# A hybrid decoder layer on one core: projections 256 tokens at a time and a pair of blocks ahead, their weights through a ring, the gate's products moved

## The chip, the cores and the metric

The kernel runs on one core of a Trainium2 chip. A core has TensorE (PE in the profile; its weight loads are PEld), VectorE (DVE), ScalarE (ACT), GpSimd (POOL) and SyncE (SP), which issues most DMA transfers. Each engine works its own instructions in a fixed order and waits on semaphores for the others. The metric is the device time of one execution in microseconds, as a median of runs. The time before is 2795.03 us (three runs, 2791.49 to 2799.54).

## The reference

One decoder layer over 2048 tokens of width 1024, in float32, with two sandwich-normalised sub-layers:

```
xn   = rms_norm(x) * g
proj = xn @ w_in                                   # 3336 columns
z, xbc, dt = SSD part (512, 1024, 8 columns)
xbc  = silu(causal_conv4(xbc));  dt = softplus(dt + bias)
y_ssd  = chunked state-space scan (8 heads of 64, 2 groups, state 128), times silu(z), group norm
p    = p_rwkv + (shift_by_one_token(p_rwkv) - p_rwkv) * mu     # 1792 columns: r, w_lo, k, v, a_lo, g_lo
S_t  = S_{t-1} * w_t + (S_{t-1} a_t) b_t + v_t k_t ;  y_t = S_t r_t   # RWKV7, 8 heads of 64, per token
h    = x + rms_norm([y_ssd ; y_rwkv] @ w_out)
y    = h + rms_norm( (silu(gate) * val) @ w_down ),  gate, val = causal_conv3(rms_norm(h) @ w_up)
```

All mixing is causal.

## The kernel before, in words

The work is written in three phases, R, S and F, that hand data to one another through DRAM: XN (the normed tokens, transposed), XC (the convolved xbc columns), YR (the RWKV output), H and HN. Every large product is done in two-term half precision: a float32 operand is split into a high and a low float16 part, and three products (high-high, high-low, low-high) are summed in PSUM. So a product over the 1024 features is 8 x 3 = 24 matmuls.

**Phase R** goes over 16 blocks of 128 tokens. For a block, `load` (L302) fetches x, norms and transposes it into `xt`, whose first three columns are the last three of the block before, and stores it to XN. The projections are 14 groups of 128 columns for RWKV (`d`, L330, weights `W`) and 8 groups for xbc (`conv`, L349, weights `WC`). All weights are split once at the start and stay in SBUF. `dense` (L200) issues the 24 matmuls; they move 129 columns for `d` (128 tokens and the one before, for the token shift) and 131 for `conv` (three before, for the 4-tap convolution). After every second group ACT and DVE take the pair out of PSUM: `d` makes a token-shift mix (L342 to L347), `conv` makes the taps (one on POOL at L362, three on DVE at L367), a tanh and a product (L372), and a store to XC.

The recurrence of a block is done in 64-token halves in matrix form: `low_rank`, `keys`, `norm` (with product nq, L412), `receptance`, `gram` (two, L443, masked into G at L447), `solve` (L451) and `transposed`; these belong to the front of the block (`f.`). `solve` inverts triangular 32 x 32 blocks: the blocks of G go to DRAM (ATd) and come back redistributed over the partitions (atl), 62 small DVE operations at L471 and L474 do the substitution, and the result goes through DRAM (XTd) to XT. The back of a block (`b.`), which runs during the next block's front, is `values`, `own`, `merge` (pw and po; its first step transposes XT into XW at L515), `update` (pu), `state` (pS, pq), `gate` and `finish` (yt).

TensorE's order is the order in which the program calls these steps: phase R runs through the step lists FIRST, SECOND, PLAN, LAST and DRAIN. The other engines' orders, and that of the DMA issues, are set by a planner with its own time estimates. In PLAN (L122) the projections `f.d.0` to `f.d.13` and `f.conv.0` to `f.conv.7` of a block are strewn among the front steps of the same block and the back steps of the block before. `merge.0` stands two groups ahead of `gram.0`.

**Phase S** goes over 16 chunks of 128 tokens (pairs of chunks share loads). For a pair, `steps`, `sums` and `flip` make the step sizes dt and their running sums (products dt at L763, acs at L795 and L806; a chain of tiny DVE operations at L774 to L790). For a chunk, `z` (L824) makes the gate's columns in four bursts of six matmuls of 512 columns; then come `begin`, `decay`, `keys`, `off`, `y`, `state`, `norm`, `o` (the output projection, four bursts of 12 at L958) and `post` (the two norms and the transposed copy hT, which goes to HN; product ht at L983). While phase R drains its last block (DRAIN, each "S" is one step of S_DRAIN), it runs chunk 0, the z bursts of chunks 0 to 3 and the steps of pairs 0 and 1. From chunk 1 on, each chunk runs S_PLAN (L100), in which a "Z" is one z burst of a later chunk (from a list that S_QUOTA deals out), and `s.steps`, `t.sums`, `t.flip` are those of a later pair. `post` of a chunk comes one chunk after its `o`.

**Phase F** is the feed-forward part, in two halves of 1024 tokens. The change doesn't touch it.

Of the kernel before, what the change touches and what calls it, by code (L numbers as in the profile page):

```python
# [7 lines left out]
F32 = mybir.dt.float32  # L8
# [46 lines left out]
class Space:  # L55
# [20 lines left out]
R_LEFT = ("sq", "kkn", "thw", "tha", "Pv", "xin", "wl", "wr", "tk", "BK", "ca cth", "raw", "xt", "wc")  # L76
R_RIGHT = (
    "cw cb mus omu w0h a0h ka5 kam tiny vr gnv gnr ss pnv pnr", "XT0 XT1 qs S0_0 S0_1 tS ysb yln tg",
    "g2 cmat tv GL WA WX xl tmp XW", "UV", "G", "BT", "atl", "Pi", "AR", "tr",
)  # L80
S_LEFT = (
    "wdt dtb Ab Db cst_s sng", "wst", "ws0", "ws1", "xt", "ws2", "ws3", "dv de dq ds dtt da nac", "sz", "th", "xbc", "R",
    "Dt", "pp rr ones3 E", "identb mnegb", "Btok", "Xdt", "Xd", "aend dec sgs sgv sgr", "ST0 ST1", "sq", "yt0",
# [12 lines left out]
S_DRAIN = """  # L96
s.steps c.z.0 c.z.1 c.z.2 c.z.3 s.sums n.z.0 s.flip c.rows n.z.1 n.z.2 n.z.3 c.begin m.z.0 c.off c.keys c.decay.0 m.z.1
c.decay.1 m.z.2 m.z.3 t.steps u.z.0 u.z.1 u.z.2 n.rows c.y u.z.3 c.state
# [5 lines left out]
S_QUOTA = (3,) * 12 + (4,) * 3  # L104
# [3 lines left out]
SPLITS = ('AV', 'AV', 'AV', 'GV')  # L108
FIRST = """
f.d.0 f.d.1 f.d.2 f.d.3 f.low_rank f.d.4 f.d.5 f.keys f.d.6 f.d.7 f.d.8 f.norm f.d.9 f.conv.0 f.receptance f.conv.1  # L110
f.conv.2 f.gram.0 f.conv.3 f.gram.1 f.solve f.conv.4 f.conv.5 f.conv.6 f.conv.7 f.transposed.0
n.load.10.11 f.transposed.1 f.d.12 f.d.13
"""
SECOND = """
f.d.0 f.d.1 b.values f.d.2 f.d.3 f.low_rank f.d.4 f.d.5 f.keys f.d.6 f.d.7 f.d.8 b.own.0 f.norm f.d.9 f.receptance
f.conv.0 f.conv.1 f.conv.2 f.conv.3 f.gram.0 b.merge.0 f.gram.1 f.solve b.merge.1 f.conv.4 b.update.0 f.conv.5 b.state.0
f.conv.6 f.transposed.0 b.own.1 f.conv.7 b.update.1 b.state.1 f.transposed.1 n.load.10.11 b.gate f.d.12 f.d.13 b.finish
"""
LAST = """
# [58 lines left out]
def norm_T(tc, K, work, psp, pstag, src, g, dst, col, sfx, between=None, junk=None):  # L178
# [6 lines left out]
    for q in range(2):  # L185
# [14 lines left out]
def dense(tc, ps, w, xt, cols):  # L200

    nc = tc.nc
    n = 0
# [1371 lines left out]
```

## Time and profile before

| | us |
|---|---|
| median of three runs | 2795.03 |
| the profiled execution | 2795.42 |
| its span, first to last instruction | 2793.4 |
| phase R's projections, first to last | 11.5 to about 1006 |
| z bursts, first to last | 1006.7 to 1436.6 |
| o products, first to last | 1077.1 to 1473.5 |
| granted clock, mean | 0.957 |

The profile is one execution. Busy times of one engine may hold overlapping instructions only once, while the mean in nanoseconds is that of one instruction with its whole pipeline; so for matmuls that follow one another the distance of their starts says what one costs. A row of the timeline gives the start, the length, the instruction and, in brackets, how long the engine sat idle before it and what ended that. A row of the waits gives the waiting instruction, the releaser, the total in us, how often, and the longest.

### The profile page before, as it was taken

Reading aid. Unit: us, or ns where it says so; the run is one execution under the profiler, and the core shown is the slowest. Engines: PE = TensorE matmul, PEld = TensorE weight load, DVE = VectorE, ACT = ScalarE, POOL = GpSimd, SP = SyncE. Lnnn points to the kernel's source line nnn. Section 1 sums busy time; section 2 is a strip of 40 time slices with the busy share of each in tenths; the row PEclk is TensorE's granted clock in tenths of the full one; section 3 lists DMA queues with packets and bytes.
Section 4 is the critical chain, followed back from the end, with each engine's and each line's share of the span. In section 5 each row is a group of like instructions: output and inputs, shape, how many; then the busy total and the mean of one; then the engine's idle time right before and its main releaser. Section 6 shows DMA issues by size and latency. Waiting matters only on the chain.

```text
span 2793.4 us, 54157 instructions
## 1 busy us (share of the span) xinstructions
PE 2533.3 (91%) x21458; PEld 1595.1 (57%) x21468; DVE 1942.4 (70%) x3711; ACT 1196.6 (43%) x2448; POOL 1237.7 (44%) x1286
## 2 busy tenths in 40 slices
PE   5898899999989989899898798989988899999998
PEld 5888888888878865455443343434433344444443
DVE  7778767777777766556767858787879744554557
ACT  5455555445555534344444444434344333132132
POOL 5234434434434423333457855657476532132234
PEclk8999999999999989999999899999999999999999
DMA  6212121221211144333355334343434633333243
GB/s 213 52 43 60 47 48 45 52 51 43 60 47 45 40 149 137 107 105 124 136 183 190 126 138 155 136 154 132 151 129 155 226 99 106 102 101 102 86 137 126
DMA packets 261278, 302.62 MB, mean 108 GB/s; under 512 B 133664, under 2 KB 168864, under 8 KB 257696
## 3 DMA queue, kind: packets, MB, share of 16 engines
q1 hardware_dynamic: 259440, 296.54, 33.4%
q8 instruction: 168, 2.75, 0.4%
q10 hardware_dynamic: 1584, 2.63, 0.3%
q14 instruction: 86, 0.70, 0.1%
HBM read 188.11 MB, written 110.99 MB: 107 GB/s over the span
## 4 chain that ended last, share of the span: by engine, by line
PE 42%; DVE 25%; POOL 11%; DMA 8%; issue 8%; ACT 4%; SPq 2%; POOLq 0%; DVEq 0%; ACTq 0%
PE u L1182 16%; PE d L1329 10%; PE d L206 4%; DVE ca L367 3%; PE o L958 3%; DVE xl L474 3%; DVE tmp L471 3%; POOL fa L1087 2%; DMA HN<-hT 2%; DMA atl<-ATd 2%; DVE a L1219 2%; POOL us L1083 1%; PE l L1410 1%; POOL p L1247 1%; DMA ATd<-G 1%
## 5 line engine op out<-in xcount | busy, mean ns | idle before, releaser
L1182 PE MATMUL u<-b,w 128*128 128x512 f16 x3696 | 820.4, 384 | 52.1 <-DVE C L1191 36.5
L1182 PEld LDWEIGHTS <-w 128*128 128x128 f16 x3696 | 365.3, 99 | 503.5 <-issue 80.5
L206 PE MATMUL d<-xt,wr 128*128 128x129 f16 x5376 | 356.3, 230 | 7.2 <-DVE xt L197 5.1
L206 PEld LDWEIGHTS <-wr 128*128 128x128 f16 x5376 | 346.0, 103 | 28.9 <-issue 23.0
L1329 PE MATMUL d<-dw,fa 128*128 128x512 f16 x1512 | 339.8, 384 | 18.3 <-DVE dw L159 17.6
L1329 PEld LDWEIGHTS <-fa 128*128 128x128 f16 x1596 | 158.1, 99 | 222.7 <-issue 34.7
L1191 DVE TENSOR_TENSOR C<-u,C 128x512 f32<-128x512 f32 x220 | 150.6, 685 | 188.6 <-PE u L1182 151.4
L206 PE MATMUL c<-xt,wc 128*128 128x131 f16 x3072 | 201.2, 223 | 0.3 <-ACT tr L344 0.3
L206 PEld LDWEIGHTS <-wc 128*128 128x128 f16 x3072 | 184.7, 98 | 5.8 <-issue 0.7
L367 DVE SCALAR_TENSOR_TENSOR ca<-rc,cw,ca 128x128 f32<-128x128 f32 x384 | 156.5, 440 | 39.9 <-POOL ca L362 38.3
L1338 DVE TENSOR_TENSOR acc<-d,acc 128x512 f32<-128x512 f32 x212 | 139.8, 682 | 57.3 <-PE d L1329 56.6
L1219 DVE SCALAR_TENSOR_TENSOR p<-C,fpar,p 128x1024 f32<-128x1024 f32 x88 | 121.8, 1384 | 70.2 <-ACT p L1217 70.1
L159 DVE SCALAR_TENSOR_TENSOR w<-us,w 128x512 f16<-128x512 f32 x132 | 121.4, 925 | 68.2 <-ACT w L158 67.1
L471 DVE TENSOR_TENSOR tmp<-atl,xl 128x60 f32<-128x60 f32 (+24 forms) x496 | 122.1, 246 | 52.2 <-DMA atl<-ATd 41.9
L1086 ACT ACTIVATE fa<-p 128x512 f16<-128x512 f32 x132 | 79.6, 624 | 177.4 <-DVE p L1223 94.1
L1087 POOL TENSOR_TENSOR fa<-p,fa 128x512 f16<-128x512 f32 x120 | 151.5, 1273 | 3.6 <-ACT fa L1086 3.6
L474 DVE TENSOR_TENSOR xl<-xl,tmp 128x60 f32<-128x60 f32 (+24 forms) x496 | 137.4, 277 | 11.8
L158 ACT ACTIVATE w<-us 128x512 f16<-128x512 f32 x132 | 80.5, 623 | 139.3 <-POOL us L1083 99.9
L1219 DVE SCALAR_TENSOR_TENSOR a<-C,fpar,a 128x1024 f32<-128x1024 f32 x88 | 128.9, 1465 | 4.5 <-ACT a L1217 1.7
L362 POOL TENSOR_SCALAR ca<-rc,cw,cb 128x128 f32<-128x128 f32 x128 | 69.7, 553 | 135.4 <-ACT rc L359 61.7
L1216 POOL COPY C<-fcarry 128x2 f32<-128x2 f32 x88 | 40.9, 467 | 158.4 <-ACT a L1217 77.3
L1221 POOL COPY fcarry<-C 128x2 f32<-128x2 f32 x88 | 34.4, 391 | 169.1 <-DVE C L1191 168.7
(318 smaller groups left out, 4583.9 us busy)
## 6 DMA issues: line engine op xcount, KB each, us to landing
UW<-w SPq DMA_DIRECT2D x154, 256.0 KB
w<-UW SPq DMA_DIRECT2D x154, 256.0 KB
us<-in_w_u_dram SPq DMA_DIRECT2D x44, 512.0 KB
DW<-dw SPq DMA_DIRECT2D x70, 256.0 KB
dw<-DW SPq DMA_DIRECT2D x56, 256.0 KB
hs<-HN SPq DMA_DIRECT2D x48, 256.0 KB
r<-in_w_d_dram SPq DMA_DIRECT2D x10, 1024.0 KB
xin<-in_x_dram SPq DMA_DIRECT2D x16, 512.0 KB
```

Of the source, the lines that this page charges most:

```text
L159: eng.scalar_tensor_tensor(out=lo, in0=src, scalar=scale, in1=hi, op0=ALU.mult, op1=ALU.subtract)
L206: nc.tensor.matmul(ps, w[:, a, kt, :], xt[:, kt, b, cols], start=n == 0, stop=n == 3 * KT - 1)
L367: V.scalar_tensor_tensor(out=acc[:, q], in0=raw[:, q, k:k + 128], scalar=cw[:, g + q, k:k + 1], in1=acc[:, q], op0=ALU.mult, op1=ALU.add)
L471: V.tensor_tensor(out=tmp[:, :m, :n], in0=atl[:, j, j + 1:32].unsqueeze(1).to_broadcast([P, m, n]), in1=xl[:, :m, j:j + 1].to_broadcast([P ...
L474: V.tensor_tensor(out=xl[:, :m, j + 1:32], in0=xl[:, :m, j + 1:32], in1=tmp[:, :m, :n], op=ALU.add)
L958: nc.tensor.matmul(self.po, l, WO[:, v, (kt + 4) % KT, ds_], start=k == 0, stop=k == 23)
L1087: eng.tensor_tensor(out=lo, in0=src, in1=hi, op=ALU.subtract)
L1182: nc.tensor.matmul(bk[at], self.w[i][:, u, k, :], self.half.b[i][:, k, v, :], start=start and n == 0, stop=n == 11, skip_group_check=True)
L1191: V.tensor_tensor(out=o, in0=ps, in1=a, op=ALU.add)
L1219: V.scalar_tensor_tensor(out=a, in0=c[:, 2 - d:1026 - d], scalar=cw[:, g, 2 - d:3 - d], in1=a, op0=ALU.mult, op1=ALU.add)
L1329: nc.tensor.matmul(ps, pairs[m].a[i][:, u, t * P:t * P + P], ws[n][m][:, v, :], start=new and m == 0 and u == v == 0, stop=m == N - 1 and ...
L1338: V.tensor_tensor(out=acc[j][:, t], in0=ps, in1=acc[j][:, t], op=ALU.add)
```

## The change

In phase R the unit is no longer a block but a pair of blocks for the projections. `load` of two blocks fills one `xt` of 256 columns. A generator (`stream`) yields the projections of all pairs as units: half of one group's product, that is four of the eight feature tiles, 12 matmuls of 256 columns. There are 44 units a pair. Tokens before the pair are no longer projected again; the last one or three columns of the raw projections are kept in `carry` and copied in front of the next pair's. Evacuation, token shift, taps and the tanh work on 256 columns. `low_rank`'s token part (WA, GL, WX) moves to the pair (`gates`).

The stream runs ahead: 30 units and one more inside a `load` are issued before block 0 begins, and each block then takes 22 units ("D" in the one PLAN, one of them inside `load` of the block four ahead). FIRST, SECOND and LAST go. In PLAN the back steps come earlier: `merge.0` stands after eight units, before `norm`, and `gram.0` and `gram.1` after five more.

Weights are no longer resident. A ring of 11 tiles ("wr") holds them. For pairs 0 and 1 they are loaded in float32 and split (each takes two tiles, fetched five groups ahead); pair 1 also stores the split tiles to DRAM (WD). From pair 2 on they are loaded split from WD, ten groups ahead. `wl` gets a fourth, zero-filled part, so that both low-rank products use 128 rows.

When the stream ends (in block 14), each "D" becomes a step of phase S: the 64 z bursts of all chunks, with `steps`, `sums` and `flip` of all pairs among them. The gated z is stored to DRAM (SZ) and loaded in `begin`. Chunk 0's remaining steps (S_FIRST) come when phase R is through; S_PLAN loses its Z, s and t steps and keeps the order of the rest.

```diff
-FIRST = ...   -SECOND = ...   -LAST = ...   -S_QUOTA = ...   -S_DRAIN = ...
+S_FIRST = """c.rows c.begin c.off c.keys c.decay.0 c.decay.1 n.rows c.y c.state"""
 S_PLAN = """
-c.begin c.decay.0 Z c.off p.norm c.keys Z c.decay.1 p.o.0.0 Z t.sums p.o.0.1 t.flip Z n.rows q.post.0 c.y c.state
-p.o.1.0 q.post.1 p.o.1.1 s.steps
+c.begin c.decay.0 c.off p.norm c.keys c.decay.1 p.o.0.0 p.o.0.1 n.rows q.post.0 c.y c.state
+p.o.1.0 q.post.1 p.o.1.1
 """
+LEAD = 30
+RING = 11
 PLAN = """
-f.d.0 f.d.1 b.values f.d.2 f.d.3 f.low_rank f.d.4 f.d.5 f.keys f.d.6 f.d.7 f.d.8 b.own.0 f.norm f.d.9 f.receptance f.conv.0 f.conv.1 b.merge.0 f.conv.2 f.gram.0 b.merge.1 f.conv.3 b.update.0 f.gram.1 f.solve f.conv.4 b.state.0 f.conv.5 f.transposed.0 b.own.1 f.conv.6 b.update.1 f.conv.7 b.state.1 f.transposed.1 n.load.10.11 b.gate f.d.12 f.d.13 b.finish
+D D b.values D f.low_rank D D f.keys D b.own.0 D D b.merge.0 f.norm D b.merge.1 f.receptance D b.update.0 D
+b.state.0 D f.gram.0 D f.gram.1 f.solve b.own.1 D D b.update.1 D f.transposed.0 D b.state.1 D f.transposed.1 D b.gate
+n.load D b.finish D
 """
 DRAIN = """
+D D b.values D D b.own.0 D D D D D D D D D D D D D b.merge.0 D D b.merge.1 D b.update.0 D D b.state.0 D b.own.1 D D
+b.update.1 D D b.state.1 b.gate D D D D D b.finish
 """
...
+        def load_w(pair, g):
+            src = w_r[g] if g < 14 else w_c[g - 14]
+            w = wk.tile([P, 2, KT, P], F16, name=f"w{pair}_{g}", tag="wr", bufs=RING)
+            if pair > 1:
+                nc.sync.dma_start(w, WD[g])
+                return w
+            st = wk.tile([P, KT, P], F32, name=f"wf{pair}_{g}", tag="wr", bufs=RING)
+            nc.sync.dma_start(st, src)
+            ...
+            V.scalar_tensor_tensor(out=lo, in0=st, scalar=WS, in1=hi, op0=ALU.mult, op1=ALU.subtract)
+            if pair == 1:
+                nc.sync.dma_start(WD[g], w)
+            return w
...
+            def units(self):
+                ...
+                for g in range(0, NG, 2):
+                    ps = psp.tile([P, 2, 256], F32, name=f"d{self.sf}_{g}", tag="mm", bufs=2)
+                    ...
+                    for q in range(2):
+                        w = self.weights(g + q)
+                        for k in (0, 4):
+                            dense(tc, ps[:, q], w, self.xt, slice(0, 256), range(k, k + 4))
+                            if q and k:
+                                self.done(g, ps)
+                            yield
+            def raw(self, g, ps, k):
+                raw = wk.tile([P, 2, 259], F32, name=f"raw{self.sf}_{g}", tag="raw", bufs=2)
+                V.tensor_copy(raw[:, :, 3 - k:3], carry[:, g:g + 2, 3 - k:3])
+                S.activation(raw[:, :, 3:259], ps, AF.Copy)
+                V.tensor_copy(carry[:, g:g + 2, 3 - k:3], raw[:, :, 259 - k:259])
+                return raw
...
+        def stream():
+            for p in pairs:
+                for n, _ in enumerate(p.units()):
+                    yield
+                    for g in range(n // 2 + 1, n // 2 + 1 + (RING // 2 if p.n < 2 else RING - 1)):
+                        if g < NG:
+                            p.fetch(g)
+                        elif p.n + 1 < PAIRS:
+                            pairs[p.n + 1].fetch(g - NG)
+        def piece():
+            if not over[0]:
+                if next(pieces, pieces) is not pieces:
+                    return
+                over[0] = True
+                for c in reversed(front):
+                    c.close()
+                next(filler)
+            next(filler)
+        for n in range(LEAD):
+            piece()
+            if n in (9, 19):
+                blocks[2 + n // 10].load(piece if n == 9 else None)
...
 # phase S
+            nc.sync.dma_start(SZ[self.n], sz)          # end of z
 ...
+            self.sz = wk.tile([P, 512], F32, name="szl" + cf, tag="sz", bufs=3)   # begin
+            nc.sync.dma_start(self.sz, SZ[self.n])
...
+    for c in chunks:
+        for g in range(4):
+            if c.c == 0 and g == 0 and c.n // 2 + 1 < blocks:
+                pairs[c.n // 2 + 1].load_x()
+            c.z(g)
+            if c.c == 0 and g == 1:
+                c.q.steps()
+            elif c.c == 1 and g == 0:
+                c.q.sums()
+            elif c.c == 1 and g == 2:
+                c.q.flip()
+            if not K.finished:
+                yield
```

More of the change, by code (lines that the diff above doesn't have):

```diff
@@ L375, in low_rank @@
[L375 to L380 removed]
+            def low_rank(self):
+                X, thw, tha, Pi, Pv = self.pair.X, self.thw, self.tha, self.Pi, self.Pv
@@ L991, in phase_S @@
     chunks = [Chunk(n) for n in range(N)]
-    gates = [(n, g) for n in range(4, N) for g in range(4)]
     def follow(n, plan):
-        left = S_QUOTA[n - 1] if n < N else 0
         for step in plan.split():
@@ L1040, in phase_S @@
             pairs[n // 2 + 1].load_b()
-        elif n % 2 and n // 2 + 2 < blocks:
-            pairs[n // 2 + 2].load_x()
         yield from follow(n, S_PLAN)
```

349 lines of the change are left out of this document (172 added, 177 removed).

## The prediction

> **What bounds the kernel now.** I read the page's share of each engine, then the stretches of the span, and then the first stretch closely, since that is where nearly all of the change lies.
>
> ```profile
> PE 2533.3 (91%) x21458; PEld 1595.1 (57%) x21468; DVE 1942.4 (70%) x3711; ACT 1196.6 (43%) x2448; POOL 1237.7 (44%) x1286
> ...
> 0.00:120.00 120.00, 83.55 (x1056) 74.99 (x1056) 92.47 (x205) 63.85 (x127) 50.06 (x52) 0.87 0.44 145
> 120.00:960.00 840.00, 763.82 (x11663) 694.31 (x11664) 628.40 (x1839) 427.88 (x1024) 341.25 (x407) 0.96 0.20 49
> 1070.00:1440.00 370.00, 336.00 (x1907) 190.73 (x1914) 232.91 (x422) 157.45 (x429) 133.58 (x150) 0.97 0.36 118
> ```
>
> Columns: stretch, length, then PE, PEld, DVE, ACT and POOL busy, granted clock, DMA share, GB/s. PE leads everywhere, but in the steady stretch of phase R it idles 76 of 840 us. One period of a 128-token block runs from one norm product (nq) to the next:
>
> ```profile
> L412 PEld LDWEIGHTS nq<-sq,cst x32: 192/192/338, 46.0 to 969.8; 128*128 128x128 f32 x32
> ...
> PE zw L388 <- DVE WX L384: 26.2, 14, 2.7
> PE yt L617 <- POOL ysb L613: 18.0, 13, 1.4
> PE pS L585 <- ACT UV L568: 13.1, 14, 1.7
> PE gr L443 <- DVE BK L427: 8.6, 13, 0.7
> PE pt L191 <- DVE xin L193: 7.9, 12, 0.7
> ...
> 298.40:358.90 60.50, 55.29 (x860) 50.52 (x858) 46.05 (x135) 31.50 (x76) 25.11 (x30) 0.97 0.20 50
> ```
>
> This is its weight load, two per block; 15 periods from 46.0 to 969.8: 61.6 us each. A single period holds 55.3 us of PE and 46.1 of DVE; PE's waits (in total, times, longest) are short and of many causes. Beside PE runs a second chain of nearly the same length, the triangular solve of a block: gram product, mask (G), two trips through DRAM, 62 small DVE operations, two more trips, transposition (XW), merge product (pw).
>
> ```profile
> 490.32 1.16 PE L443 MATMUL gr<-AR,BK 64*128 64x128 f32 x16
> ...
> 494.61 0.68 DVE L447 TENSOR_TENSOR G<-gr,cst 128x512 f32<-128x512 f32 x1
> 502.60 0.19 DVE L471 TENSOR_TENSOR tmp<-atl,xl 128x31 f32<-128x31 f32 x1 [2.38 <-DMA atl<-ATd]
> 532.60 0.25 DVE L474 TENSOR_TENSOR xl<-xl,tmp 128x8 f32<-128x8 f32 x1
> 540.17 0.43 DVE L515 STREAM_TRANSPOSE XW<-XT 32x256 f32<-32x256 f32 x1 [0.76 <-DMA XT<-XTd]
> ...
> 538.34 1.54 PE L206 MATMUL d<-xt,wr 128*128 128x129 f16 x24
> 539.72 2.98 PE L206 MATMUL c<-xt,wc 128*128 128x131 f16 x48
> 542.63 0.69 PE L522 MATMUL pw<-XW,G 32*32 32x32 f32 x32
> 545.50 1.16 PE L443 MATMUL gr<-AR,BK 64*128 64x128 f32 x16 [0.67 <-DVE BK L427]
> 549.80 1.16 PE L443 MATMUL gr<-AR,BK 64*128 64x128 f32 x16
> ```
>
> From the end of gr (491.5) to the end of XW (540.6) are 49.1 us: 3.8 to G's end, 7.3 to the data, 30.2 of solve (that includes some 14 us of other DVE work), 7.7 back. pw starts only 2.0 us after it. So PE sets the period now, and the solve is the next thing late, by 2 us.
>
> **The change, part by part.**
>
> *Wider projections.* Start to start, 24 products of 129 columns take 1.38 us (538.34 to 539.72), 57.5 ns each; 48 of 131 take 2.91 (to 542.63), 60.6. A block has 14 x 24 and 8 x 24: 31.0 us. Products of 256 columns don't occur in this form; a z burst of 512 columns does:
>
> ```profile
> 1219.86 1.47 PE L830 MATMUL z<-ws,xs 128*128 128x512 f16 x6
> 1221.16 1.03 PE L895 MATMUL pf<-ST,xbc 128*128 128x256 f32 x4
> ```
>
> 1.30 us for six, 217 ns each. A straight line from (129, 57.5) to (512, 217) gives 110 for 256; bounds: 108.5 (half of 512) and 115 (twice 129). I take 109: one unit ("D", 12 products) 1.31 us, 22 units a block 28.8. Saved: 2.2 us a block at full clock, not the half that halving the instructions suggests. The Trainium skill, "TensorE: Matmul & The Clock Gate" (Back-to-back issue gap), gives 81 ns for 128 columns and 131 for 512 in a stream with weight loads; by it the saving, an estimate, would be some 270 us in all. The trace contradicts both figures.
>
> The other PE work stays: 55.3 us at a clock of 0.97 are 53.6 at full clock, 31.0 of them projections and so 22.6 recurrence. They become 51.4, or 54 at the stretch's mean clock of 0.96 (28.8 and 22.6, divided by it: 30 and 23.5).
>
> *Waits.* The wait on WX (1.8 us a block) goes, since WX is made a pair ahead. The other waits stay or grow, because one D (1.38 us at this clock) now stands where 1.5 to 2.9 us stood: about 1 on UV, 2 on pt and 0.5 on G; I count 3.5 (bounds 1 and 7). PE alone would then need 57.5.
>
> *The order of the steps.* From the new PLAN I add PE's time from the end of the second gram to the next merge.0: 17 D (23.3) and pt's wait (2) beside most of the recurrence. From merge.0 to the second gram's end stand 5 D (6.9), nq, pw, po, pu, pS, pq and two gr (0.6 to 1.1 us each, 7.4 together; gr is 545.50 to 546.59) and 1.5 of waits, 15.8 us. Now it is 8.3 (542.63 to 550.9). What is left of the recurrence, 16, makes the first part 41.7. So the solve's chain may take 41.7 us before PE waits at merge.0, where every later product of both blocks and of the pair ahead is queued behind it.
>
> *The solve's chain after.* DVE gets lighter:
>
> ```profile
> L367 DVE SCALAR_TENSOR_TENSOR ca<-rc,cw,ca 128x128 f32<-128x128 f32 x327 | 135.3, 445 | 34.3 <-POOL ca L362 32.8
> L372 DVE SCALAR_TENSOR_TENSOR ca<-ct,ca 128x256 f32<-128x256 f32 x55 | 23.0, 419 | 0.9 <-ACT ct L371 0.5
> L346 DVE SCALAR_TENSOR_TENSOR tk<-raw,mus,tk 128x128 f32<-128x128 f32 x54 | 17.6, 346 | 29.3 <-ACT tk L344 29.3
> ...
> L284 DVE SCALAR_TENSOR_TENSOR wr<-wst,wr x14: 1193/1215/2059, 10.7 to 43.8; 128x1024 f16<-128x1024 f32 x14
> ```
>
> 24 taps of 128 columns (135.3/327 = 0.41) become 12 of 256 (0.42 by the next row): 4.9 us less at most, 1.5 less if one counts the 0.26 us at which taps follow each other. 14 shifts of 0.35 become 7 of 0.42, and 22 tiny carry copies a pair come in. In the solve's own stretch the other work falls from 14 to about 10. Chain: G 2, data 7.3, solve 26, back 8.1, XW 0.4: 43.7. Bounds: 41 (the other work lands outside the solve) to 48 (nothing gained). The period is 43.7 and 15.8: **59.5 us**, against 61.6. PE then waits 2 at merge.0. Fifteen periods: -31.5 us.
>
> *Weights through the ring.* 22 loads of 512 KB a pair, 11.5 MB in 119 us, 97 GB/s on top of 49; the first 40 us carry 299 GB/s:
>
> ```profile
> 0.00:40.00 40.00, 21.17 (x206) 18.56 (x207) 24.32 (x39) 23.38 (x41) 17.31 (x20) 0.87 0.82 299
> ...
> SPq L477 <- DVE xl L474: 17.2, 2, 9.9
> ...
> 11.49 0.27 PE L206 MATMUL d<-xt,wr 128*128 128x129 f16 x1 [0.67 <-ACT xt L196]
> ```
>
> The bandwidth is there. SP's queue waits in order, 9.9 us at a time for the solve's end (the row covers two blocks); the new loads, their waits for a free slot, the 22 WD stores, the 16 SZ stores and the solve's 16 small transfers all pass it. Ten tiles ahead are 20 units, over 40 us of PE, which covers such a wait (without that cover it is PE that waits the 9.9); the cost in time is zero unless the solve's transfers wait behind a load (a rival below). Weights are split again in the second pair: 22 x 1.2 us of DVE, some 5 us of it in two solves that are critical; it lies inside the front's term.
>
> *Front.* The first product starts about as before (11.5; xin_1 comes ahead of the weights). 31 units pass first: 4 narrow ones at 1.5 and 27 at 1.38, 43 us; transposes 4; then 8 units and low_rank, 16. The first nq falls at 75 rather than 46: **+29**. In return the last blocks have z units to run.
>
> *z.* 64 bursts of 1.3 us; 16 ran in the drain and 48 in phase S. All now run in blocks 14 and 15 and the drain. From nq(15) to the drain's end: 15.8, then 48 to merge.0 (26 z units among other products, longer than the chain), then 31, and 3 for the first z, which waits for its tokens: 98, before 99.8 (969.8 to 1069.6): **-2**.
>
> *Phase S.* One chunk takes 25.2 us now (px, four per chunk, 15 chunks):
>
> ```profile
> L848 PE MATMUL px<-ident_s,xbc x60: 272/273/329, 1069.6 to 1423.1; 128*128 128x128 f32 x60
> ...
> PE acs L795 <- DVE da L790: 20.8, 6, 4.8
> PE ht L983 <- DVE xi L978: 9.4, 6, 2.4
> ...
> 1191.62 5.11 DMA HN<-hT
> 1201.78 2.37 DVE sz L838
> 1205.12 1.04 ACT hT L976 x2
> 1207.40 1.30 DVE xi L978
> 1208.74 0.65 PE ht L983 x4
> 1215.08 2.59 PE o L958 x12
> ...
> 1193.33 0.60 ACT L961 ACTIVATE m<-o 128x512 f32<-128x512 f32 x1 [1.99 <-PE o L958]
> ```
>
> Its 48 bursts (62 us) and the wait on da (20.8) go. But the chain from the last o product (ends 1193.3) through m, which waits for HN's transfer out of the same buffer, and xi to ht takes 15.4 us and stays: 14.1 without sz (2.37), which holds L976 back by 1.3. PE's 336 us over 14.7 chunks are 22.9 each; less z's 4.2 and 0.8 of steps they are 17.9, of which 8.9 follow ht to the end of the next o (1217.7). So 9 us of PE lie over a chain of 14.1, and a chunk takes 14.1 and 8.9, 23: -2.2 a chunk over 15, -33. Chunk 0, which the drain covered, now stands bare between the drain and chunk 1: a third of a chunk's PE work and the decay's exponentials, +8 (bounds 5 and 15). The added sz load hides under the chunk before it; without that cover it is about 2 us. **-25**.
>
> Sum: +29 - 31.5 - 2 - 25 = -29.5, against the profiled execution's 2795.4 (span 2793.4 and 2.0 around it; 0.4 above the median): **2766 us**.
>
> **Rivals.**
>
> *The solve's chain becomes the bound and lengthens.* 299 GB/s moves a 512 KB load in 1.75 us, and four trips of the solve can each stand behind one, besides SP's issue time. At 48 us of chain the period is 63.8: +64, **2830**, slower. It decides from a period of 62, a chain of 46.3 (38 us above the forecast). For: only 2 us of slack now, and 7.5 us more PE work behind merge.0. Against: less DVE work. The Trainium skill, "DMA: Bandwidth & Descriptors" (Queues, rings and completion order), says that each DMA engine consumes descriptors in ring order; that speaks against this change. No run here shows it with such loads.
>
> *PE stays the bound.* Chain 41.7 or less, period 57.5: another -30, **2736**. For: DVE is only 46 of 61.
>
> *Phase S shrinks by all of its z work.* The ht chain finds cover: 62 and 20.8 go rather than 33: -50, **2716**. Against: the 9.4 us of waits on xi that stand there already.
>
> *It does nothing.* The projections were hidden enough, the period stays near 61.2, the front is paid by phase S: +25, **2791**.
>
> **How the numbers follow.** Forecast 0.30; the long chain 0.27; PE-bound 0.20; S in full 0.08; nothing 0.15. A run of this kernel tells 0.3% (8 us) from no change: faster 0.58, same 0.15, slower 0.27. The range reaches from S in full to the long chain, where its bound lies: 2712 to 2832; the forecast's own is 2745 to 2787.
>
> **What would show it.** Units of 12 products at 1.3 to 1.4 us; no wait on WX; PE's wait at pw on XW, about 2 us a block (none: PE-bound; over 6: the slow rival); solve from first tmp to last xl near 26; chunks of 23 us with ht waiting 5 on xi; nq first at 75. The forecast is wrong if the period is outside 57 to 62 or a chunk of S is below 21.

## The result and the profile after

The changed kernel takes 2959.19 us (median of four runs, 2956.86 to 2965.59), the kernel before 2797.07 beside it: a ratio of 1.0586, with a 95% interval of 1.0561 to 1.0611. It is 5.9% slower. The profiled execution has a span of 2955.4 us, 162.0 more than the 2793.4 of before.

The page's first part of the changed kernel:

```profile
PE 2525.8 (85%) x17292; PEld 1509.9 (51%) x17292; DVE 1915.2 (65%) x3533; ACT 1207.9 (41%) x2217; POOL 1245.8 (42%) x1229
```

PE's and DVE's busy times fell a little, by 7.5 and 27 us, but PE is busy for 85% of the span rather than 91%. So the time didn't go into work; it went into waiting. Where, the stretches of the changed kernel tell (stretch, length, then PE, PEld, DVE, ACT and POOL busy, granted clock, DMA share, GB/s):

```profile
0.00:120.00 120.00, 87.08 (x752) 73.71 (x753) 89.78 (x149) 70.57 (x111) 54.22 (x50) 0.91 0.71 251
120.00:1000.00 880.00, 691.25 (x7473) 573.43 (x7472) 564.87 (x1570) 393.80 (x758) 307.32 (x322) 0.88 0.44 134
```

In phase R, PE now idles 189 of 880 us, where it idled 76 of 840, and the granted clock fell from 0.96 to 0.88. The first and last starts of nq and of px (four a chunk) give the landmarks, as before:

```profile
L466 PE MATMUL nq<-sq,cst x32: 592/1061/1222, 88.5 to 1124.5; 128*128 128x512 f32 x32
...
L928 PE MATMUL px<-ident_s,xbc x60: 272/273/474, 1259.6 to 1580.6; 128*128 128x128 f32 x60
```

| | before | after | change | predicted change |
|---|---|---|---|---|
| start to the first nq | 46.0 | 88.5 | +42.5 | +29 |
| 15 periods of phase R | 924.2 | 1036.0 | +111.8 | -31.5 |
| last nq to chunk 1 of phase S | 99.4 | 135.1 | +35.7 | +6 |
| chunk 1 to chunk 15 | 353.5 | 321.0 | -32.5 | -33 |
| the rest | 1370.3 | 1374.8 | +4.5 | 0 |
| span | 2793.4 | 2955.4 | +162.0 | -29.5 |

In the kernel before, the row of nq is

```profile
L412 PE MATMUL nq<-sq,cst x32: 592/595/1222, 46.0 to 970.2; 128*128 128x512 f32 x32
```

(the prediction read its weight load, to 969.8). The period is 69.1 us, not 59.5, on average over the fifteen; between the ends of block 2's and block 12's second grams (259.7 and 940.7) it is 68.1. PE's waits in the changed kernel, from 120 to 1120 and then from 1260 to 1600, in phase S (total, times, longest):

```profile
PE pw L576 <- DVE XW L569: 123.9, 26, 23.2
...
PE z L907 <- DVE xl L528: 15.9, 1, 15.9
PE zw L442 <- ACT UV L557: 12.8, 6, 2.7
PE pS L639 <- ACT UV L622: 12.0, 3, 4.4
...
PE bc L955 <- ACT aend L963: 33.7, 14, 4.2
PE ht L1063 <- DVE xi L1058: 19.1, 9, 6.8
```

The wait on WX is gone. In the block shown of before, XW was ready 2 us before PE came to pw, so PE did not wait there. Now it waits at merge.0 for the solve, 124 us in 14 blocks: 24 and 14 us in the first two, then about 4 and 11 in turn. Two solves show why. This is the timeline of the changed kernel, for block 4 and block 5: the first and last of the solve's operations, G ahead of it and XW behind it, and then PE's products.

```profile
404.81 0.19 DVE L525 TENSOR_TENSOR tmp<-atl,xl 128x31 f32<-128x31 f32 x1 [4.31 <-DMA atl<-ATd]
432.89 0.17 DVE L528 TENSOR_TENSOR xl<-xl,tmp 128x8 f32<-128x8 f32 x1
441.55 0.42 DVE L569 STREAM_TRANSPOSE XW<-XT 32x256 f32<-32x256 f32 x1
...
459.82 0.68 DVE L501 TENSOR_TENSOR G<-gr,cst 128x512 f32<-128x512 f32 x1
467.69 0.19 DVE L525 TENSOR_TENSOR tmp<-atl,xl 128x31 f32<-128x31 f32 x1 [2.87 <-DMA atl<-ATd]
503.80 0.16 DVE L528 TENSOR_TENSOR xl<-xl,tmp 128x8 f32<-128x8 f32 x1
510.63 0.43 DVE L569 STREAM_TRANSPOSE XW<-XT 32x256 f32<-32x256 f32 x1 [0.16 <-DMA XT<-XTd]
...
510.53 0.31 PE L576 MATMUL pw<-XW,G 32*32 32x32 f32 x2 [9.81 <-DVE XW L569]
512.11 2.08 PE L466 MATMUL nq<-sq,cst 128*128 128x512 f32 x2
532.89 1.18 PE L497 MATMUL gr<-AR,BK 64*128 64x128 f32 x16
```

The solve of block 4 takes 28.2 us, that of block 5 36.3, and so it goes on, even and odd. From XW's end (511.1) to that of the second gram (534.1) there are 23.0 us, from 442.0 to 459.2 in the block before 17.2. What differs between the two solves is the convolution. The stretches of the two solves, of the changed kernel, for instructions on `ca` alone (length, then DVE, ACT and POOL busy):

```profile
404.80:433.00 28.20, 0.00 (x0) 0.00 (x0) 0.00 (x0) 0.88 0.41 131
467.70:504.00 36.30, 6.95 (x13) 1.24 (x2) 2.90 (x4) 0.94 0.51 166
```

DVE's taps and products of the convolution take 7 us of the second solve and none of the first; the difference between the two is 8. The convolution's four evacuations of a pair follow its 32nd, 36th, 40th and 44th unit; with 30 units and one in a `load` issued ahead, all four fall into the even block's list, behind its 1st, 5th, 9th and 13th unit, and the first two of these meet the solve of the odd block before, which is still running.

### The profile page after: what moved, and what is told of

Its sections match the earlier page's. It is cut to its first block, busy times and chain, and to the rows that moved or that the text cites. A ratio compares the mean times of both kernels' runs of the same rounds, so it can differ in the third digit from the quotient of the medians.

```text
span 2955.4 us, 45492 instructions
## 1 busy us (share of the span) xinstructions
PE 2525.8 (85%) x17292; PEld 1509.9 (51%) x17292; DVE 1915.2 (65%) x3533; ACT 1207.9 (41%) x2217; POOL 1245.8 (42%) x1229
## 4 chain that ended last, share of the span: by engine, by line
PE 37%; DVE 12%; POOL 11%; DMA 6%; issue 4%; ACT 3%; SPq 1%; POOLq 0%; DVEq 0%; ACTq 0%
PE u L1262 15%; PE d L1409 9%; PE o L1038 3%; POOL fa L1167 2%; PE d L199 2%; POOL us L1163 1%; PE z L907 1%; DMA HN<-hT 1%; POOL p L1327 1%; DVE xl L528 1%; DVE tmp L525 1%; PE l L1490 1%; DVE w L153 1%; POOL m L1053 1%; PE py L988 1%
## 5 line engine op out<-in xcount | busy, mean ns | idle before, releaser
L1262 PEld LDWEIGHTS <-w 128*128 128x128 f16 x3696 | 364.7, 99 | 497.9 <-issue 73.7
L199 PE MATMUL d<-xt,w 128*128 128x256 f16 (+1 forms) x4272 | 536.8, 284 | 3.6 <-DVE w L284 3.2
L199 PEld LDWEIGHTS <-w 128*128 128x128 f16 x4272 | 425.8, 102 | 97.1 <-issue 26.8
L525 DVE TENSOR_TENSOR tmp<-atl,xl 128x60 f32<-128x60 f32 (+24 forms) x496 | 129.7, 262 | 65.9 <-DMA atl<-ATd 54.8
L634 POOL TENSOR_TENSOR tS<-S,Pi 64x256 f32<-64x256 f32 x64 | 45.7, 714 | 282.5 <-DVE S L644 280.1
L576 PE MATMUL pw<-XW,G 32*32 32x32 f32 x512 | 20.0, 230 | 125.3 <-DVE XW L569 123.9
L907 PE MATMUL z<-ws,xs 128*128 128x512 f16 x384 | 94.2, 388 | 21.1 <-DVE xl L528 15.9
L1038 PE MATMUL o<-wo,yr 128*128 128x512 f16 x384 | 104.6, 430 | 3.7 <-DMA yr<-YR 3.7
```

Source lines behind the costliest of these rows:

```text
L199: nc.tensor.matmul(ps, w[:, a, kt, :], xt[:, kt, b, cols], start=kt == n == 0, stop=kt == KT - 1 and n == 2)
L525: V.tensor_tensor(out=tmp[:, :m, :n], in0=atl[:, j, j + 1:32].unsqueeze(1).to_broadcast([P, m, n]), in1=xl[:, :m, j:j + 1].to_broadcast([P ...
L907: nc.tensor.matmul(self.pz, self.q.xt[:, 2 * g + k, v, self.cs], W[g][:, k, u, :], start=g == k == u == v == 0, stop=g == 3 and k == 1 and ...
L1038: nc.tensor.matmul(self.po, l, WO[:, v, (kt + 4) % KT, ds_], start=k == 0, stop=k == 23)
L1262: nc.tensor.matmul(bk[at], self.w[i][:, u, k, :], self.half.b[i][:, k, v, :], start=start and n == 0, stop=n == 11, skip_group_check=True)
```

## The experiments

Single executions stand beside one of the kernel before on the same chip (2792.3 for the first four; 2784.1 to 2791.6 on the other chips). A total that differs by less than 0.3% (8 us) says nothing by itself; there the rows inside the traces are read.

**The convolution left out (e1_noconv).** Taps (POOL and DVE), tanh and product of the convolution are not made in this kernel; the raw projections go to XC.

```diff
-                acc = wk.tile([P, 2, 256], F32, name=f"ca{self.sf}_{g}", tag="ca", bufs=2)
-                ... (taps on POOL and DVE, th on ACT, product on DVE)
-                nc.sync.dma_start(XC[self.n][:, g:g + 2, :], acc)
+                nc.sync.dma_start(XC[self.n][:, g:g + 2, :], raw[:, :, 3:259])
```

> The changed kernel with the convolution left out: taps, tanh and product are not made, the raw projections go to XC. Theory A (the evacuations of the convolution, 256 columns at once on DVE and ACT, fall into the solve of every odd block, since the stream runs 31 units ahead): the stretch from first tmp to last xl is 26 to 29 us in both parities, the period 62 to 63 instead of 69.0, the time 2959 - 15 x 6.5 = 2860. Rival B (the ring's loads delay the solve's four trips through DRAM): the odd solve chains stay 5 us longer than the even ones, the time stays above 2930.

2866.07 us. In its timeline, two solves that follow each other, first and last operation:

```profile
436.21 0.19 DVE L512 TENSOR_TENSOR tmp<-atl,xl 128x31 f32<-128x31 f32 x1 [3.02 <-DMA atl<-ATd]
461.30 0.17 DVE L515 TENSOR_TENSOR xl<-xl,tmp 128x8 f32<-128x8 f32 x1
...
497.63 0.19 DVE L512 TENSOR_TENSOR tmp<-atl,xl 128x31 f32<-128x31 f32 x1 [6.83 <-DMA atl<-ATd]
524.62 0.18 DVE L515 TENSOR_TENSOR xl<-xl,tmp 128x8 f32<-128x8 f32 x1
```

25.3 and 27.2 us: the large alternation is gone. The row of nq is 85.3 to 1036.6, 63.4 us a period. Theory A gave 2860 and holds closely; 85 of the 112 us that phase R lost go with the convolution. The rest is in the first two periods and the last, below.

**The ring's loads left out (e2_noring).** From pair 2 on the products read five tiles of pair 1, and nothing is loaded: the weights are wrong there.

```diff
             def weights(self, g):
+                if self.n > 1:
+                    return pairs[1].w[17 + g % 5]
```

> The changed kernel without the ring's loads from pair 2 on: the products of pairs 2 to 7 read five weight tiles of pair 1 (wrong weights, the same work on every engine but the DMA queues). Theory A: the two trips of the solve get at most 1 us shorter together, the period stays 68 to 69, the time 2940 to 2960. Rival B (loads ahead of the solve's transfers in the rings): the trips fall from 8 and 8 us to about 6.5 and 7, the period by 3 us or more, the time to 2915 or less.

2937.73 us; DMA's share falls from 0.44 to 0.20 between 120 and 1000, and the period from 69.1 to 67.8:

```profile
L468 PE MATMUL nq<-sq,cst x32: 592/1061/1222, 87.5 to 1104.8; 128*128 128x512 f32 x32
```

So the loads cost 1.3 us a block, slightly above what theory A allowed and far below the 3 of rival B. From G's end to the solve's first operation the mean over blocks 2 to 11 fell from 8.1 us to 6.8; from the solve's end to XW's it stayed at 7.9. The prediction's slow rival, four trips that each stand behind a 1.75 us load, is not what happened. The Trainium skill, "DMA: Bandwidth & Descriptors" (Queues, rings and completion order), has each DMA engine take descriptors in ring order. At most 1.3 us a block can come of that here; whether ring order is the cause no run shows.

**Another lead (e3_lead25).**

```diff
-LEAD = 30
+LEAD = 25
```

> One number changed: the stream runs 25 units ahead before block 0, not 30, so the four evacuations of the convolution fall on units 6, 10, 14 and 18 of the even blocks instead of 1, 5, 9 and 13. Theory A: no convolution is left in the solve of the odd blocks (their stretch falls from 36 to 28), one or two come into that of the even ones (28 to 31 to 34); the period is 64 to 67, the first nq some 9 us earlier, the time 2880 to 2925. Rival B: only the front moves, 2950.

2940.99 us: a miss for theory A's figure. The timeline shows that the mechanism is right and the size was not, for blocks 5 and 6:

```profile
460.79 0.19 DVE L525 TENSOR_TENSOR tmp<-atl,xl 128x31 f32<-128x31 f32 x1 [7.57 <-DMA atl<-ATd]
485.91 0.17 DVE L528 TENSOR_TENSOR xl<-xl,tmp 128x8 f32<-128x8 f32 x1
523.26 0.19 DVE L525 TENSOR_TENSOR tmp<-atl,xl 128x31 f32<-128x31 f32 x1 [0.90 <-DMA atl<-ATd]
557.19 0.16 DVE L528 TENSOR_TENSOR xl<-xl,tmp 128x8 f32<-128x8 f32 x1
```

Now the odd block has 25.3 us and the even one 34.1. The collision moved to the other parity, as theory A says, but again two evacuations lie in one solve: four of them span 12 units of a block's 22, and a solve with its trips leaves fewer free.

**Another order (e4_plan).** The same steps; norm, both grams and the solve come ahead of the other block's merge.0, so that the stretch between them is no longer added to the solve's chain.

```diff
-D D b.values D f.low_rank D D f.keys D b.own.0 D D b.merge.0 f.norm D b.merge.1 f.receptance D b.update.0 D
-b.state.0 D f.gram.0 D f.gram.1 f.solve b.own.1 D D b.update.1 D f.transposed.0 D b.state.1 D f.transposed.1 D b.gate
-n.load D b.finish D
+f.low_rank D f.keys D b.values D D b.own.0 D f.norm D D f.receptance D D f.gram.0 D f.gram.1 f.solve D b.merge.0 D
+b.merge.1 D b.update.0 D b.state.0 D b.own.1 D b.update.1 D f.transposed.0 b.state.1 D f.transposed.1 D b.gate
+n.load D b.finish D
```

> The changed kernel with another order of the same steps in PLAN: low_rank and keys at the start, norm and both grams and the solve ahead of the other block's merge.0, so that the stretch from merge.0 to the second gram's end (20 us, which adds to the solve's chain in the period) is gone from the loop. Theory A: the chain of 47 to 52 us then runs beside 56 us of PE, PE's wait at pw goes (under 1 us a block), the clock stays at 0.95, the period is 57.5 to 60: 2959 - 15 x 10 = 2790 to 2825. Rival C (DVE as a whole has become too slow, its 45 us a block and its waits set the period): the period stays above 64, the time above 2880.

2839.28 us, 120 less than the change. Two starts of nq in its timeline, ten blocks apart:

```profile
281.18 2.08 PE L466 MATMUL nq<-sq,cst 128*128 128x512 f32 x2 [3.17 <-ACT sq L459]
860.94 1.13 PE L466 MATMUL nq<-sq,cst 128*128 128x512 f32 x2 [1.82 <-ACT sq L459]
```

And PE's wait at pw from 120 to 930:

```profile
PE pw L576 <- DVE XW L569: 17.4, 2, 16.7
```

The steady period is 58.0 us. The wait at pw occurs only in block 0. Two things changed at once. The chain, now 41 to 49 us from the second gram's end to XW's end in blocks 2 to 13, runs beside PE instead of in turn with it. And the convolution no longer meets the solve: two of its operations (1.2 us) lie in an even block's solve and none in an odd block's, where 13 (7 us) lay before, and the solves take 28 and 24 us in turn where they took 28 and 36. e1_noconv, with the old order and no convolution at all, had come to 2866.07 us; how much of the 120 us belongs to which of the two no run parts. The expected 2790 to 2825 was missed by what lies outside the steady blocks: the first periods, where pair 1's weights are split a second time, and the end.

**Three edits around it (e5_once, e6_zpool, e7_early)**, each on the kernel just told: the weights split once (pair 0 stores them, pair 1 loads); the z weights' split moved from DVE to POOL and ACT; the front of block 0 called inside the lead.

```diff
-            if pair > 1:                                   # e5: also the store at pair == 0, the longer lead from pair 1
+            if pair > 0:
-            split_w(tc, W[g][:, :, 0], W[g][:, :, 1], st, V)       # e6
+            split_p(W[g][:, :, 0], W[g][:, :, 1], st)              # POOL scales, ACT rounds, POOL subtracts
+        EARLY = {10: begin, low_rank; 13: keys; 21: norm; 25: receptance}   # e7, after these units of the lead
```

> The reordered kernel (e4_plan), with the weights split once: pair 0 stores the split tiles and pair 1 already loads them. Theory A (the second split costs DVE 22 x 1.2 us in the solves of blocks 0 and 1, which makes the early periods long: 158.5 to 236.7 between two second grams, 78 us, against 58): those periods fall to about 62, the time from 2839 to 2815 to 2825. Rival D (the front is bound by its DMA, share 0.68 to 0.72 in the first 120 us, and stores put there cost as much as they save): first nq 8 us or more later, 2835 to 2845.

> The reordered kernel (e4_plan), with the split of the z weights on POOL and ACT in place of DVE. Theory A (the first z burst waits 17.5 us because its weights' low parts stand behind the solve in DVE's order): the wait falls under 5 us, the time from 2839 to 2822 to 2828. Rival E (it waits for the loads or for room, and DVE only comes last): the wait stays over 12, the time 2835 or more.

> The reordered kernel (e4_plan), with low_rank, keys, norm and receptance of block 0 called inside the lead (after its units 10, 13, 21 and 25) instead of after it. Theory A (the first nq waits 10.4 us for a chain of ACT and DVE that nothing covers): that wait goes, the second gram of block 0 ends at 90 instead of 105, the time falls by 10 to 15 to 2824 to 2829. Rival D (the front is bound by weights and DMA): the lead gets longer by what the wait gives back, 2835 or more.

2832.25, 2846.29 and 2836.99 us, with 2791.64 before. These totals lie within 8 us of e4_plan's, so none gave the gain expected. In the first, the first nq comes at 98.2 rather than 84.7, as rival D said; the period between the second grams of blocks 1 and 2, 78 us in e4_plan (158.5 to 236.7), became 70 (159.0 to 229.2) and not 62. So the second split, with the shorter lead of its loads, costs some 8 us there, and the rest of that long period has another cause, which was not sought. The second was a miss: the wait at the first z stayed and now has another name,

```profile
PE z L912 <- DMA xs<-XN: 17.4, 1, 17.4
```

so the burst waits for its tokens. SP issues their load at 958.13, 12 us into that wait, behind the solve's transfers and the store of the last convolution; the burst starts 5.1 us later. By the program the tokens' place in memory comes free only when the stream has ended; how much of the wait is that and how much SP's order was not tried. The third is a miss too: nq comes at 60.7 and block 0's second gram ends at 93.4, as theory A said (105.4 in e4_plan), but that of block 2 ends at 236.3, where e4_plan had 236.7. So the 12 us were not lost in the lead, as rival D had it, but in the two blocks after it, while pair 1's weights are loaded and split.

**All three, and norm and grams somewhat later (e8_all).**

```diff
+f.low_rank D f.keys D b.values D D b.own.0 D D f.norm D D D f.receptance D D f.gram.0 D f.gram.1 f.solve b.merge.0 D
```

> The three edits of e5_once, e6_zpool and e7_early together, and norm one unit and gram.0 two units later in the order than in e4_plan (PE's waits there for sq and for DVE at gr, 26 and 42 us between 120 and 1000). If the gains add (18, 14, 12, and 20 of the 68): 2775; if the work behind them is bound elsewhere, 2800 or more. Steady periods 57 to 58.

2809.99 us: the gains did not add to 2775. The steady period is right:

```profile
271.84 1.12 PE L466 MATMUL nq<-sq,cst 128*128 128x512 f32 x2 [1.63 <-ACT sq L459]
842.53 1.02 PE L466 MATMUL nq<-sq,cst 128*128 128x512 f32 x2
```

57.1 us, against 61.6 before. So the steady blocks are 4.5 us shorter than in the kernel before. The wider projections were to save 2.2 of that; what is theirs and what the new order's was not parted. What is left of the loss lies at both ends.

**Phase S's wait at the decay (e9_s_bc).** Held back are also the first six steps after the switch to phase S; norm, grams and merge.0 come two units later still.

```diff
-            bc = bank(f"bc{self.cf}{g}", "bc")
+            bc = bank(f"bc{self.cf}{g}", ("bc", "mm")[g])
```

> Three things that can be read apart by place. Phase S: the second decay's product goes to the bank that the z bursts have left free (mm), not to the one that the first still holds; PE's wait there is 33.7 us in 14 chunks. If that wait is on S's path, a chunk falls from 22.9 to 20.5 to 21.5 and the last o comes 20 to 30 us sooner; if the chain from o through the two norms to ht sets S, as the prediction has it, ht's wait grows by as much as bc's falls and a chunk stays at 22.5 to 23. End of phase R: after the switch to phase S the first six steps are held back, so that PE does the recurrence while the first z's tokens and weights are loaded; the wait at the first z falls from 17 to 18 to 8 to 11. Phase R: as e8_all with norm, grams and merge.0 two units later again; PE's wait for sq at nq falls from 24 to under 8, steady period 57. Sum: 2810 less 25, 7 and 10 is 2768; without the gain in S 2793.

2886.81 us. The row of px, four a chunk:

```profile
L937 PE MATMUL px<-ident_s,xbc x60: 272/273/477, 1152.8 to 1506.9; 128*128 128x128 f32 x60
```

In PE's waits of this kernel from 1180 to 1500 the one for aend is gone, and this stands first:

```profile
PE ht L1072 <- DVE xi L1067: 54.1, 13, 5.0
```

The wait moved to ht whole, and a chunk takes 25.3 us ((1506.9 - 1152.8)/14) rather than 22.9. The chain from o's end to ht kept its length (13.4 us in the changed kernel, 13.2 here, means of 13 chunks), so that chain sets phase S. What got longer is the stretch from ht to the end of the next o, from 9.8 to 12.6 us. The traces show why. Here is one chunk of this kernel, then one of the changed kernel in which PE had not waited at ht:

```profile
1314.07 1.11 PE L1072 MATMUL ht<-ident_s,xi 128*128 128x128 f32 x4 [4.35 <-DVE xi L1067]
1314.98 3.51 PE L997 MATMUL py<-Xdt,Dt 128*128 128x64 f32 x16
...
1409.90 0.60 PE L1063 MATMUL ht<-ident_s,xi 128*128 128x128 f32 x4
1410.34 1.90 PE L988 MATMUL py<-Xdt,Dt 128*128 128x64 f32 x16
```

One wait of over 4 us in place of two shorter ones left PE at half speed behind it; the granted clock from chunk 1 to chunk 15 is 0.84, and 0.92 in the changed kernel. The wait for the first z's tokens is gone from the list, as expected. Phase R got worse, 62.6 us a period over all fifteen where e8_all had 60.8, with 65.1 us of waits at gr for DVE's BK up to 900: moving norm and the grams two units later shifted DVE's part of norm into its work for the solve, the reading goes, and that was not tried apart.

**Phase R's end.** The steps held back, on e8_all without the POOL split; then, in a second kernel, also 14 of the 64 z bursts left to phase S, one a chunk.

```diff
+            if hold[0]:
+                hold[0] -= 1
+                return
             next(filler)
...
-c.begin c.decay.0 c.off p.norm c.keys c.decay.1 ...
+c.begin c.decay.0 c.off p.norm c.keys Z c.decay.1 ...
```

> e8_all without its POOL split of the z weights (e6_zpool showed that the first burst waits for its tokens' load, not for the split), and with the first six steps after the switch to phase S held back, so that PE does the recurrence of block 14 while that load runs. Theory A: the wait of 18.3 us at the first z falls under 8 and the time from 2810 to 2797 to 2803. Rival F (the recurrence steps that move forward wait in their own chain instead, and the six held bursts are only done later): 2806 or more.

> e10_hold with 14 of the 64 z bursts given back to phase S, one a chunk ahead of the second decay, where PE waits 2.5 us a chunk for ACT (34.8 us in 14 chunks). This asks what moving the z products is worth. If that wait is free room (theory A: a chunk is set by the chain from o to ht), a chunk stays at 23.2 and the drain gets 14 x 1.3 = 18 us shorter: 15 to 20 below e10_hold. Rival G (the bursts push the chain from o to ht back, as the order did in e9_s_bc): a chunk grows by 1 us or more, and the time is that of e10_hold or above.

2792.71 and 2777.43 us, with 2784.09 before on that chip. In the first, the long wait at the first z is gone. But of its 17 us against e8_all 13 lie ahead of the last projection's end (898.4 against 911.7), where nothing was held back and which stays unexplained, and e8_all ran on a chip where the kernel before took 7.5 us more. Only 4 us lie behind that point: the recurrence steps that moved forward wait in their own chain instead, as rival F said (2.4 us at pu, 2.3 at pS), and the products between their waits run at half speed (pu 1.97 us, 1.14 elsewhere). In the second,

```profile
L938 PE MATMUL px<-ident_s,xbc x60: 272/273/475, 1069.7 to 1403.6; 128*128 128x128 f32 x60
```

chunk 1 begins 24.4 us earlier than in e10_hold (1094.1), and a chunk takes 23.9 us rather than 22.9: of 1.3 us that a burst costs phase S hides 0.4 in this execution, and the drain gives back more than the 14 bursts' 18. Both expectations were right in part.

**More bursts, and the better one timed.**

```diff
+c.begin c.decay.0 Z c.off p.norm c.keys Z c.decay.1 ...
```

> As e10_late with 28 of the 64 z bursts in phase S, two a chunk (one behind the first decay, one ahead of the second), and the step list of the drain cut to what is left. If the room in a chunk of S holds only one burst (e10_late: PE's wait at the second decay is all but gone, a chunk went from 22.9 to 23.9), a chunk becomes 25 or more and the time stays at 2775 to 2785; if the chain from o to ht still hides it, 2765. In the drain the last solve's chain (40 us) loses its cover: a wait at pw of 5 us or more.

> e10_late again, timed against the kernel before: one execution each gave 2777 and 2784. 0.990 to 0.996 if that holds; 1.0 if it was the scatter of single executions.

With 28 bursts in phase S: 2799.05 us, 1.0004 times before (0.9988 to 1.002). A chunk takes 26.0 us, and the bare chunk 0 and drain give only 12 back; the wait at pw that was expected in the drain did not come. With 14: 2779.74 us against 2796.59, a ratio of 0.9939 (0.992 to 0.9958). In its trace a chunk takes 24.4 us (px, four a chunk, from 1069.0 to 1410.5 for chunks 1 to 15), so how much of a burst phase S hides, 0.4 us or nothing, stays open. A version of the change with another order, the weights split once, six steps held back and a part of the z products returned beats the kernel before by 0.6%.

## Why the prediction was wrong, and where it was right

*Right.* One unit of 12 products costs what the straight line gave: two in a row last 2.78 us and one 1.48, so 1.30 each.

```profile
461.21 2.78 PE L199 MATMUL d<-xt,w 128*128 128x256 f16 x24
517.30 1.48 PE L199 MATMUL d<-xt,w 128*128 128x256 f16 x12
```

That is 108 ns for 256 columns, with a weight load each. The wait on WX went; the ring's bandwidth was there. Phase S's chunk is 22.9 us where 23 was said, and its limit, the chain to ht, held in e9_s_bc. Part of that figure is luck: the chain is 13.4 us and not 14.1, and the stretch behind ht 9.8 and not 8.9, because PE is at half speed behind some waits; and of the 5 us of wait said of ht 1.4 a chunk are there and 2.4 at the second decay. The form of the sum was right too: PE in turn with the solve's chain, with pw as the place to look.

*The step that failed is the solve's chain, 43.7 us, inside the period.* These are its parts in the changed kernel, worked out from the rows of G, tmp, xl, XW and gr in the timeline:

| blocks 2 to 11, mean us | forecast | even blocks | odd blocks | all |
|---|---|---|---|---|
| gram's end to G's end | 2 | 1.6 | 1.3 | 1.5 |
| to the first tmp (there through DRAM) | 7.3 | 8.6 | 7.7 | 8.1 |
| solve, first tmp to last xl | 26 | 28.0 | 36.2 | 32.1 |
| to XW's end (back through DRAM) | 8.5 | 8.4 | 7.3 | 7.9 |
| chain | 43.7 | 46.6 | 52.5 | 49.5 |
| XW's end to the next second gram's end | 15.8 | 16.6 | 20.6 | 18.6 |
| period | 59.5 | 63.1 | 73.1 | 68.1 |

First, "in the solve's own stretch the other work falls from 14 to about 10". That spread the evacuations evenly over a pair. They come in one clump, and half of it lands in one solve. In the even blocks the other work on DVE is 11 us and the solve 28; in the odd ones it is 18 to 21 us, 7 of them the convolution's, and the solve 36. The upper bound of 48, "nothing gained", left out that a clump could be worse than before. e1_noconv prices the convolution at 5.7 us a period, and with it out of the way the sum nearly comes out: over the same blocks the solve is 26.6 us, the chain 45.0 and the other stretch 16.8. The starting point was off as well: the block read, with a solve of 30.2 us, was one of the three shortest of blocks 2 to 13 of the kernel before, whose solves take 32.0 on average and up to 33.0. One tap was also dearer than the row that I took for it:

```profile
L385 DVE SCALAR_TENSOR_TENSOR ca<-raw,cw,ca 128x256 f32<-128x256 f32 x168 | 83.7, 538 | 9.3 <-POOL ca L380 9.3
```

538 ns, not 420. The two trips through DRAM were sized right, 16.0 us together where 15.8 were said.

Second, the stretch from merge.0 to the second gram, 15.8 us. It measures 16 to 17 us in most blocks and 22 to 24 behind the solves of blocks 3, 5 and 9. In all of them the products right after pw ran at half speed (nq 2.08 us for two, 1.13 in the reordered kernel's row at 860.94), which the sum had left out. What the three long ones have besides shows in the rows of PE and of ACT, of the changed kernel, three behind the solve of block 4 and the others behind that of block 5:

```profile
443.01 2.08 PE L466 MATMUL nq<-sq,cst 128*128 128x512 f32 x2
452.41 0.69 PE L639 MATMUL pS<-UV,BT 128*64 128x64 f32 x16
453.03 1.14 PE L647 MATMUL pq<-UV,G 64*64 64x64 f32 x16
...
524.79 1.12 PE L639 MATMUL pS<-UV,BT 128*64 128x64 f32 x16 [3.53 <-ACT UV L622]
525.85 1.97 PE L647 MATMUL pq<-UV,G 64*64 64x64 f32 x16
...
523.50 0.63 ACT L389 ACTIVATE ct<-ca 128x512 f32<-128x512 f32 x1 [5.29 <-DVE ca L385]
524.15 0.59 ACT L622 ACTIVATE UV<-pu 64x512 f32<-64x512 f32 x1
```

PE waits 3.53 us at pS for UV. In the block before, UV started as soon as pu had ended (451.10). Here pu ended at 519.9, but in ACT's order UV stands behind the tanh of the convolution's third evacuation, and that waited 5.29 us for the taps. Behind PE's wait the products run at half speed once more. From nq's start to the second gram's end the long stretch has 5.8 us more than the short one: 3.3 of it ahead of pS, 2.5 behind. Blocks 3 and 9 show the same rows, with waits of 4.1 and 4.4 us at pS; in e1_noconv, without the tanh, no block waits there. So this too is the clump.

Third, the prediction put the second split of the weights, "some 5 us of it in two solves", inside the front's term. The solves of blocks 0 and 1 take 37.4 and 38.3 us, and their periods are 78.4 and 73.4. e5_once shows the split's part in the other order: without it the solve of block 0 takes 31.0 us, with it (e4_plan) 50.3. The last period, 78.5 us, holds the first z's wait.

The prediction's condition, "the forecast is wrong if the period is outside 57 to 62", was the one that failed, and its sign to look for, over 6 us of wait at pw, is what the trace shows. The slow rival named the right place, a chain over 46.3 us, with a wrong cause (loads ahead of the trips) and too small a price: its 48 us of chain are 49.5 on average, but the stretch behind the chain grew too, and so did the front and the end.

*The front*, 88.5 rather than 75: PE had come to nq at 78.6, near what was said, but then waited 9.9 us for the keys' chain on ACT. e7_early shows that hiding this wait is worth almost nothing to the whole: what it gains ahead of block 0's second gram is gone two blocks later.

*The end*, 135.1 rather than 106. The first z waited 15.9 us, not 3, but that wait (1066.6 to 1082.5) lies ahead of the last nq, in the fifteenth period. Behind the last nq, chunk 0 took 20.3 us bare (1239.3 to 1259.6), not 8, and the drain 115 us, not 98. The bursts were counted right, 26 ahead of merge.0; but the wait on da, which was to go from phase S, came along into the drain with 10.4 us in 5 waits, and 4.1 us of waits for ACT at z joined it. Nor had the bursts cost phase S their whole length: 48 of them, 62 us, left it, and it got 32.5 shorter. The first 14 given back to it (e10_late) cost 0.9 us a chunk and took 1.7 each off the end; the next 14 (e11_late28, beside e12_late14) cost 1.6 a chunk and took off 0.85 each.

## What to carry to other kernels

Where a loop's period is one engine's chain plus a stretch of another's, look first whether the order can put the two side by side; here another order, which also took the clump out of the solve, was worth more (120 us) than the work saved (2.2 us a block). Batching two blocks' work also batches its evacuations: place the clump on the timeline of each engine that takes it, look what stands behind it in that engine's order, and price the worst block, not the mean. And work that seems moved for free may have been the filler of a wait where it stood.

## What the runs showed of the hardware

After a wait of 9.81 us at pw, PE ran at half speed: nq's two products took 2.08 us, where 1.13 is seen without such a wait, and nq's median over the run is 1061 ns for one product, 595 before. The unit at 517.30 is at full speed again, 6.8 us after work resumed. The Trainium skill, "TensorE: Matmul & The Clock Gate" (What's actually happening), says that the array drops to half rate after an idle window of about 3.4 us and returns after a busy one; the trace agrees for this wait and for the 3.53 us at pS. But shorter waits can do it too: in e4_plan's row at 281.18 nq took 2.08 us after 3.17 us, and in phase S of the changed kernel, after 2.42 us at the second decay (1400.95), twelve products of o took 5.30 us, where they take 2.75 at full speed. A long wait of PE so costs more than its own length, and one wait of 4 us in a chunk cost more than two of 2 (e9_s_bc).

A load of a function table on ACT takes 1.28 us. In the long stretch norm has one load more than in the short one, because the convolution's tanh (L389, 502.15) had displaced the table that L454 had loaded ahead at 497.17. It cost nothing: it lay beside nq's products, and sq started 2.18 us after nq where it had started 2.12 us after it in the block before.

```profile
445.13 0.69 ACT L467 ACTIVATE sq<-nq,tiny 128x512 f32<-128x512 f32 x1 [1.24 <-PE nq L466]
...
502.15 1.28 ACT L389 ACT_TABLE_LOAD   x1
...
513.00 1.28 ACT L467 ACT_TABLE_LOAD   x1
514.29 0.69 ACT L467 ACTIVATE sq<-nq,tiny 128x512 f32<-128x512 f32 x1
```
